# Probabilities times values by three split passes in the sparse attention, and eight steps of the adaptive-norm stream moved to the output projection

## The chip, the cores and the metric

The kernel runs on one core of one Trainium2 chip. The time is that of the device, in microseconds (us), median of several runs. The engines are called as in the profile: PE (TensorE, matrix products), PEld (its weight loads), DVE (VectorE), ACT (ScalarE), POOL (GpSimd) and SP, whose queue starts most DMAs.

## What is computed

One decoder layer over 512 tokens of width 2048, all in float32. Cut to what matters here:

```python
mod = silu(c) @ w_ada + b_ada            # six vectors of 2048: shift, scale, gate, twice
h = rms_norm(x) * (1 + sc_a) + sh_a
proj = h @ w_in                          # q, k, v of A; indexer; latents of B; two gates
score = sum_h relu(qi_h . ki) * wi_h     # indexer, 16 heads of 64; top 128 keys a row
p = softmax(where(selected, q . k * scale, -inf))
o_a = p @ v                              # mixer A: 8 heads of 128, v shared by 4 heads
o_b = causal attention                   # mixer B (MLA): 8 heads
y = (sigmoid(g_a) * (o_a @ w_pa) + sigmoid(g_b) * (o_b @ w_pb)) @ w_o
x = x + gt_a * y
x = x + gt_f * conv_ffn(rms_norm(x) * (1 + sc_f) + sh_f)
```

## The kernel before

Activations lie with 128 channels or tokens on the partitions and 512 tokens or channels along a row; a tile of that size is a slot, and 81 slots are handed out and given back by `get` and `put`. Products of activations with weights are made by split: each float32 operand becomes a high part in the reduced format fp32r and a low part, the rest (`split`: a copy on ACT, a subtraction on DVE), and `mm3` adds three fp32r passes, high by high, high by low and low by high (lines 166 to 168). Plain float32 products stand where an operand is used only once or twice: queries by keys (line 1023), and probabilities by values (line 813).

The stages in order of time: the combined input projection in quarters, to about 200 us; indexer and the rest of the projection, to about 420 us; mixer A, to about 570 us; gates, to 770; mixer B and the branch projections `w_pa` and `w_pb`, to 1077; the output projection `w_o`, to 1255; then the feed-forward network, the second half of the time.

**The indexer** (`index_heads`) takes three blocks of 128 query rows, of 256, 384 and 512 keys. Each block has eight calls of `two_rows` (line 638): two heads of 64 channels, in the upper and the lower half of the array, three passes each, so six half-height matmuls, which must keep their order. Around them PE works on the passes of the projection.

**Mixer A** loops over eight heads, one step out of phase: `attend_p` makes logits and softmax of a head, `attend_pv` transposes the probabilities of the head before (10 transposes, line 805), copies them out of PSUM (ACT and DVE by turns, lines 810 and 808), and multiplies them with the values, four matmuls of 512, 384, 256 and 128 columns (line 813). Between, `fill` gives PE one step of the gate projection at a time (24 passes of 512 columns), and calls `tick` after it.

**The stream of `w_ada`**: shift, scale and gate of the later sub-layers are sums over `w_ada`, made in 16 blocks of 8 steps, 128 steps in all. A step (`ada_load`, `ada_add`) loads two tiles of 256 KB by SP (line 837) and adds them, scaled, into an accumulator by two DVE instructions (lines 856 and 858). A `ticker` makes steps at a rate per call: in mixer A 1 and then 2 for each head, 27 in all; 20 each in the gates, with `w_pa` and with `w_pb`; in the output projection 1.25 (`TO`) for each of 32 calls, 40 in all. A finished block is summed over partitions by two passes with ones (`flush_cols`, lines 906 and 907).

The order on each engine is not the order of the code: a scheduler sets it when the kernel is built, by its own estimate of times and by priorities. Each engine then runs its queue in that order.

## Time and profile before

| | |
|---|---|
| median of 3 runs | 2592.22 us (2591.07 to 2593.68) |
| the profiled execution | 2595.53 us, of which its span is 2593.7 us |
| PE, DVE, ACT busy | 99%, 84%, 48% of the span |
| TensorE clock granted | 1.00 from 225 us to the end |

A matmul's record runs from its start to the modelled end of its pipeline, so records of one engine overlap. How fast PE works is read from start to start.

### The profile page before, as it was taken

The page shows a single profiled execution, that of the slowest core. Times are in us where ns is not written, and L with a number is a line of the kernel's source. Part 1 is how long each engine was busy: PE and PEld are TensorE (multiplying, and loading weights), DVE is VectorE, ACT ScalarE, POOL GpSimd, SP SyncE. Part 2 cuts the span into 40 slices and gives each one's busy share as a digit, 9 for nine tenths or more (in the row PEclk, how much of TensorE's full clock was granted, in tenths as well). Part 3 has the DMA queues.
Part 4 walks back from the last instruction along what each step waited for, and adds up shares of the span by engine and source line. Part 5 has one row for each costly group of instructions (what it writes and reads, how often), then busy time and mean ns, then how long its engine had stood idle before and what let it go on. Part 6 is the DMA issues. An engine that isn't in the chain of part 4 may idle for free.

```text
span 2593.7 us, 45167 instructions
## 1 busy us (share of the span) xinstructions
PE 2578.3 (99%) x17392; PEld 2341.9 (90%) x17392; DVE 2177.7 (84%) x3487; ACT 1241.1 (48%) x1949; POOL 371.3 (14%) x671
## 2 busy tenths in 40 slices
PE   9999999999999999999999999999999999999999
PEld 8887787779998877888889999999999999999999
DVE  6976995788878767876979989999989998989887
ACT  5322444344445535322545555555555555665554
POOL 1000011010023224200100000000000024414120
PEclk9999999999999999999999999999999999999999
DMA  9943136745685569966424334434344358868663
GB/s 342 362 155 110 48 100 190 228 151 175 203 269 166 161 209 352 320 230 226 154 81 156 128 122 130 141 120 133 126 150 136 126 169 230 225 167 228 155 204 116
DMA packets 216444, 466.41 MB, mean 180 GB/s; under 512 B 23930, under 2 KB 65556, under 8 KB 216228
## 3 DMA queue, kind: packets, MB, share of 16 engines
q1 hardware_dynamic: 170404, 344.93, 41.7%
q0 software_dynamic: 45792, 118.59, 15.2%
q8 instruction: 136, 2.23, 0.4%
q14 instruction: 80, 0.66, 0.1%
q10 hardware_dynamic: 32, 0.01, 0.0%
HBM read 398.16 MB, written 65.27 MB: 179 GB/s over the span
## 4 chain that ended last, share of the span: by engine, by line
PE 94%; issue 2%; DMA 2%; DVE 1%; ACT 1%; POOL 0%; SPq 0%; POOLq 0%; ACTq 0%; DVEq 0%
PE bank L1218 18%; PE bank L1220 18%; PE bank L1219 18%; PE bank L166 12%; PE bank L168 11%; PE bank L167 11%; PE bank L638 1%; PE bank L813 1%; PE bank L1366 1%; DMA raw<-in_w_ada 1%; PE bank L349 1%; PE bank L805 0%; DMA slot<-in_x 0%; DMA slot<-in_w_ada 0%; PE bank L1023 0%
## 5 line engine op out<-in xcount | busy, mean ns | idle before, releaser
L1218 PE MATMUL bank<-slot,whl 128*128 128x256 f32 x3920 | 1098.4, 281 | 3.1 <-ACT slot L1099 1.2
L1219 PE MATMUL bank<-slot,whl 128*128 128x256 f32 x3920 | 1097.0, 281 | 0.0
L1220 PE MATMUL bank<-slot,whl 128*128 128x256 f32 x3920 | 1084.9, 281 | 1.1 <-DVE whl L154 1.1
L1218 PEld LDWEIGHTS bank<-slot,whl 128*128 128x128 f32 x3920 | 737.3, 188 | 5.5 <-ACT slot L1099 2.3
L1219 PEld LDWEIGHTS bank<-slot,whl 128*128 128x128 f32 x3920 | 739.2, 189 | 0.2
L1220 PEld LDWEIGHTS bank<-slot,whl 128*128 128x128 f32 x3920 | 731.3, 188 | 1.6 <-DVE whl L154 1.5
L154 DVE TENSOR_TENSOR whl<-raw,whl 128x1024 fp32r<-128x1024 f32 (+2 forms) x560 | 607.8, 1088 | 126.9 <-ACT whl L153 121.6
L153 ACT ACTIVATE whl<-raw 128x1024 fp32r<-128x1024 f32 (+2 forms) x560 | 530.8, 949 | 357.9 <-PE bank L1219 187.9
L145 ACT ACTIVATE whl<-raw 128x1024 fp32r<-128x1024 f32 (+4 forms) x182 | 187.2, 1031 | 357.3 <-PE bank L168 182.8
L1095 DVE TENSOR_TENSOR raw<-raw 128x1024 f32<-128x1024 f32 (+2 forms) x320 | 347.1, 1085 | 3.6 <-DMA raw<-in_w_ups 1.3
L146 DVE TENSOR_TENSOR whl<-raw,whl 128x1024 fp32r<-128x1024 f32 (+4 forms) x182 | 215.6, 1187 | 111.9 <-ACT whl L145 111.1
L167 PE MATMUL bank<-whl,slot 128*128 128x512 f32 (+2 forms) x768 | 295.5, 385 | 0.0
L168 PE MATMUL bank<-whl,slot 128*128 128x512 f32 (+2 forms) x768 | 294.4, 386 | 0.0
L166 PE MATMUL bank<-whl,slot 128*128 128x512 f32 (+2 forms) x768 | 290.5, 389 | 1.5 <-DVE slot L1295 0.8
L167 PE MATMUL bank<-slot,whl 128*128 128x512 f32 (+1 forms) x656 | 263.5, 402 | 0.0
L166 PE MATMUL bank<-slot,whl 128*128 128x512 f32 (+1 forms) x656 | 261.3, 405 | 0.7 <-ACT slot L1548 0.7
L168 PE MATMUL bank<-slot,whl 128*128 128x512 f32 (+1 forms) x656 | 257.5, 401 | 0.0
L1101 ACT ACTIVATE slot<-bank 128x256 f32<-128x256 f32 x192 | 73.8, 385 | 210.5 <-PE bank L1220 210.5
L166 PEld LDWEIGHTS bank<-whl,slot 128*128 128x128 f32 x768 | 144.3, 188 | 31.0 <-issue 2.1
L168 PEld LDWEIGHTS bank<-whl,slot 128*128 128x128 f32 x768 | 144.3, 188 | 29.7 <-issue 2.2
L167 PEld LDWEIGHTS bank<-whl,slot 128*128 128x128 f32 x768 | 144.4, 188 | 29.0 <-issue 2.0
L858 DVE SCALAR_TENSOR_TENSOR slot<-slot,c_act,slot 128x512 f32<-128x512 f32 x203 | 150.8, 747 | 21.2 <-DMA slot<-in_w_ada 19.2
(296 smaller groups left out, 2774.7 us busy)
## 6 DMA issues: line engine op xcount, KB each, us to landing
slot<-in_w_ada SPq DMA_DIRECT2D x344, 256.0 KB, 5.3
raw<-in_w_ups SPq DMA_DIRECT2D x160, 512.0 KB, 3.6
raw<-in_w_in SPq DMA_DIRECT2D x50, 512.0 KB, 3.6
raw<-in_w_down SPq DMA_DIRECT2D x64, 384.0 KB, 4.0
raw<-in_w_down SPq DMA_DIRECT2D x64, 320.0 KB, 4.2
slot<-f POOLq DMA_DIRECT2D x154, 128.0 KB, 4.7
f<-slot POOLq DMA_DIRECT2D x66, 256.0 KB, 5.2
raw<-in_w_gs SPq DMA_DIRECT2D x32, 512.0 KB, 4.4
```

What stands on the lines that cost most here:

```text
L145: A.activation(hi, raw[:, :w], AF.Copy)
L146: last["lo"] = V.tensor_tensor(lo, raw[:, :w], r32(hi), ALU.subtract)
L153: return (A.activation(dst_hi, src, AF.Copy), V.tensor_tensor(dst_lo, src, r32(dst_hi), ALU.subtract))
L154: V.tensor_tensor(dst_lo, src, r32(dst_hi), ALU.subtract))
L166: PE.matmul(o, lh, rh, start=first, stop=False)
L167: PE.matmul(o, lh, rl, start=False, stop=False)
L168: PE.matmul(o, ll, rh, start=False, stop=last)
L858: V.scalar_tensor_tensor(acc, ts[i], c_act[:, k:k + 1], acc, op0=ALU.mult, op1=ALU.add)
L1095: V.tensor_tensor(o[:, :W], a[:, :W], b[:, :W], op)
L1218: PE.matmul(o, wh[:, ks], rh, start=first and k == 0, stop=False, skip_group_check=True)
L1219: PE.matmul(o, wh[:, ks], rl, start=False, stop=False, skip_group_check=True)
L1220: PE.matmul(o, wl[:, ks], rh, start=False, stop=last, skip_group_check=True)
```

## The change

The values of mixer A are split once into a high and a low part (`va`), and the tiles that held keys and values are given back at once. The transposed probabilities are split too, as they leave PSUM, into one set of three high and three low tiles for all heads, where before two heads had a set each of plain tiles. The four plain products of a head become twelve fp32r passes through `mm3`. Mixer B, which calls the same `attend_pv`, keeps the plain products. For heads 5 to 8 of the loop the first `fill` makes no step of the stream and the second makes one in place of two; `TO` goes from 1.25 to 1.5, which is 12 steps for each of the four column blocks of the output projection in place of 10.

```diff
-    TO=1.25,
+    TO=1.5,
...
+    va = ([getr(), getr()], [getr(), getr()])
+
+    def va_part(e, tb):
+        return va[e][tb // 2][:, (tb % 2) * 256:(tb % 2) * 256 + 256]
...
+        split(va_part(0, tb), va_part(1, tb), t[:, 256:512])
...
+    put(*kva)
...
-        att["t"] = [get() for _ in range(5)]
+        att["t"] = [getr() for _ in range(3)] if parts else [get() for _ in range(5)]
+        att["l"] = [getr() for _ in range(3)] if parts else []
...
+        if att["l"]:
+            pt, pl = [quad([*att[n][0:2], None, None, att[n][2]], 0) for n in "tl"]
+        else:
+            pt, pl = quad(att["t"], i), None
...
-            if kc % 2:
+            if pl:
+                last["cp"] = split(d, pl[3 - kc], b[:, :n])[1]
+            elif kc % 2:
...
-            PE.matmul(ob[:, kc * P:], vf(kc), pt[3 - kc], start=kc == 0, stop=kc == 3)
+            if pl:
+                mm3(ob[:, kc * P:], *vf(kc), pt[3 - kc], pl[3 - kc], kc == 0, kc == 3)
+            else:
+                PE.matmul(ob[:, kc * P:], vf(kc), pt[3 - kc], start=kc == 0, stop=kc == 3)
...
-    attend_bufs()
+    attend_bufs(True)
...
-        fill(1, 1)
+        fill(1, hd < 5)
...
-        fill(1, 2)
+        fill(1, 2 if hd < 5 else 1)
```

The built programs differ in order from the indexer to the end of the output projection; from the products with a unit matrix that spread the second norm (line 1533 before) PE's order is the same. Lines behind the first edits stand some lines later in the new program (858 before is 874 now, 1023 is 1039).

PE in mixer A, the products of the first head, between passes of the gate projection (whose rows name whl). Before:

```order
L813 MATMUL bank_73<-slot_3014,slot_409 128x512
L167 MATMUL bank_67<-slot_1007,whl 128x512
L168 MATMUL bank_67<-slot_1006,whl 128x512
L166 MATMUL bank_67<-slot_1011,whl 128x512
L1023 MATMUL bank_71<-slot_352,slot_130 128x384
L167 MATMUL bank_67<-slot_1012,whl 128x512
L813 MATMUL bank_73<-slot_3015,slot_412 128x384
L813 MATMUL bank_73<-slot_3600,slot_418 128x256
L813 MATMUL bank_73<-slot_3015,slot_280 128x128
```

Now, from its second product on:

```order
L167 MATMUL bank_73<-slot_3586,slot_2142 128x384
L168 MATMUL bank_73<-slot_3615,slot_2144 128x384
L166 MATMUL bank_73<-slot_3576,slot_2143 128x256
L167 MATMUL bank_73<-slot_3587,slot_2143 128x256
L168 MATMUL bank_73<-slot_3576,slot_2145 128x256
L166 MATMUL bank_73<-slot_3615,slot_2143 128x128
L167 MATMUL bank_73<-slot_3586,slot_2143 128x128
L168 MATMUL bank_73<-slot_3615,slot_2145 128x128
L1039 MATMUL bank_70<-slot_352,slot_2509 128x512
```

Four plain matmuls have become twelve passes. Between the first head's last transpose and its first product stand 21 gate passes, where there were 16.

PE in the indexer's last block (line 638, half-height, between passes of the projection), the third and fourth of its calls. Before:

```order
L638 MATMUL bank_72<-slot_1836,slot_2532 128x512
L638 MATMUL bank_71<-slot_1836,slot_2532 128x512
L638 MATMUL bank_72<-slot_1835,slot_1852 128x512
L638 MATMUL bank_71<-slot_1835,slot_1852 128x512
L638 MATMUL bank_70<-slot_1835,slot_2532 128x512
L638 MATMUL bank_73<-slot_1835,slot_2532 128x512
L638 MATMUL bank_70<-slot_1836,slot_2532 128x512
L638 MATMUL bank_73<-slot_1836,slot_2532 128x512
L638 MATMUL bank_70<-slot_1835,slot_1852 128x512
L638 MATMUL bank_73<-slot_1835,slot_1852 128x512
L168 MATMUL bank_66<-whl,slot_1327 128x512
```

Now the third of them:

```order
L168 MATMUL bank_66<-whl,slot_1332 128x512
L638 MATMUL bank_72<-slot_1835,slot_1866 128x512
L166 MATMUL bank_67<-whl,slot_1326 128x512
L638 MATMUL bank_71<-slot_1835,slot_1866 128x512
L638 MATMUL bank_72<-slot_1836,slot_1866 128x512
L638 MATMUL bank_71<-slot_1836,slot_1866 128x512
L638 MATMUL bank_72<-slot_1835,slot_2547 128x512
L638 MATMUL bank_71<-slot_1835,slot_2547 128x512
L167 MATMUL bank_67<-whl,slot_1326 128x512
```

Two calls that stood in one run of twelve now stand apart, and a full-height pass stands behind the first matmul of each, as in the four calls after them, so in six of the block's eight; before, three stood like that.

DVE in the last column block of the output projection, with the subtraction that makes each weight tile's low part (line 146) and the stream's additions between. Before:

```order
L146 TENSOR_TENSOR whl<-raw,whl 128x1024
L858 SCALAR_TENSOR_TENSOR slot_344<-slot_8785,c_act,slot_344 128x512
L858 SCALAR_TENSOR_TENSOR slot_344<-slot_8021,c_act,slot_344 128x512
L146 TENSOR_TENSOR whl<-raw,whl 128x1024
L858 SCALAR_TENSOR_TENSOR slot_344<-slot_6717,c_act,slot_344 128x512
L858 SCALAR_TENSOR_TENSOR slot_344<-slot_6745,c_act,slot_344 128x512
L146 TENSOR_TENSOR whl<-raw,whl 128x1024
```

Now, as far from the block's end:

```order
L146 TENSOR_TENSOR whl<-raw,whl 128x1024
L874 SCALAR_TENSOR_TENSOR slot_97<-slot_7145,c_act,slot_97 128x512
L872 TENSOR_SCALAR slot_280<-slot_6779,c_act 128x512
L874 SCALAR_TENSOR_TENSOR slot_97<-slot_7146,c_act,slot_97 128x512
L874 SCALAR_TENSOR_TENSOR slot_97<-slot_8847,c_act,slot_97 128x512
L874 SCALAR_TENSOR_TENSOR slot_280<-slot_6807,c_act,slot_280 128x512
L874 SCALAR_TENSOR_TENSOR slot_97<-slot_8083,c_act,slot_97 128x512
L874 SCALAR_TENSOR_TENSOR slot_280<-slot_7145,c_act,slot_280 128x512
L146 TENSOR_TENSOR whl<-raw,whl 128x1024
```

Between the last five subtractions of line 146 ahead of the block's results stood 2, 2, 5 and 5 additions; now 7, 3, 5 and 5.

## Rows read from the trace of the kernel before

**Rows 1.** The page: engines' busy time, and the chain that ended last.

```profile
PE 2578.3 (99%) x17392; PEld 2341.9 (90%) x17392; DVE 2177.7 (84%) x3487; ACT 1241.1 (48%) x1949; POOL 371.3 (14%) x671
PE 94%; issue 2%; DMA 2%; DVE 1%; ACT 1%; POOL 0%; SPq 0%; POOLq 0%; ACTq 0%; DVEq 0%
```

**Rows 2.** Waits of PE: line, releaser and its line, us in total, times, longest.

```profile
PE bank L166 <- DVE slot L1295: 0.8, 1, 0.8
...
PE bank L813 <- DVE slot L808: 0.2, 1, 0.2
```

**Rows 3.** Stretches: from:to length; busy PE, PEld, DVE, ACT, POOL; clock, DMA share, GB/s.

```profile
424.00:500.00 76.00, 75.84 (x336) 58.11 (x335) 62.14 (x143) 29.79 (x66) 5.92 (x11) 1.00 0.79 250
553.00:600.00 47.00, 47.00 (x210) 37.68 (x210) 43.54 (x82) 22.44 (x36) 4.30 (x8) 1.00 0.38 119
1077.00:1255.00 178.00, 178.00 (x782) 144.18 (x781) 129.15 (x175) 48.22 (x69) 4.72 (x8) 1.00 0.71 238
```

**Rows 4.** Order of time, PE, mixer A: start, us, engine, line, names, shape, count.

```profile
443.86 1.46 PE L813 MATMUL bank<-slot,slot 128*128 128x384 f32 x6
445.16 1.02 PE L1023 MATMUL bank<-slot,slot 128*128 128x512 f32 x2
...
457.62 1.02 PE L813 MATMUL bank<-slot,slot 128*128 128x512 f32 x2
...
458.48 0.81 PE L1023 MATMUL bank<-slot,slot 128*128 128x384 f32 x2
```

**Rows 5.** Order of time, PE: passes of 256 columns; plain products of one column.

```profile
1400.03 0.28 PE L1220 MATMUL bank<-slot,whl 128*128 128x256 f32 x1
1400.15 0.28 PE L1218 MATMUL bank<-slot,whl 128*128 128x256 f32 x1
...
80.14 0.95 PE L349 MATMUL bank<-c_act,slot 128*128 128x1 f32 x8
80.95 0.48 PE L168 MATMUL bank<-whl,slot 128*128 128x512 f32 x1
```

**Rows 6.** Order of time, PE, the indexer's last block.

```profile
315.98 0.40 PE L167 MATMUL bank<-whl,slot 128*128 128x512 f32 x1
316.30 1.66 PE L638 MATMUL bank<-slot,slot 64*128 64x512 f32 x12
...
318.23 0.40 PE L166 MATMUL bank<-whl,slot 128*128 128x512 f32 x1
...
321.29 0.40 PE L167 MATMUL bank<-whl,slot 128*128 128x512 f32 x1
321.62 0.49 PE L638 MATMUL bank<-slot,slot 64*128 64x512 f32 x1
322.04 0.51 PE L168 MATMUL bank<-whl,slot 128*128 128x512 f32 x1
322.48 0.97 PE L638 MATMUL bank<-slot,slot 64*128 64x512 f32 x5
...
323.72 0.40 PE L167 MATMUL bank<-whl,slot 128*128 128x512 f32 x1
323.95 0.39 PE L168 MATMUL bank<-whl,slot 128*128 128x512 f32 x1
324.18 0.39 PE L166 MATMUL bank<-whl,slot 128*128 128x512 f32 x1
324.50 0.96 PE L638 MATMUL bank<-slot,slot 64*128 64x512 f32 x6
...
325.73 0.40 PE L168 MATMUL bank<-whl,slot 128*128 128x512 f32 x1
```

**Rows 7.** By line, DVE: count, ns min/median/max, first and last start, forms.

```profile
L858 DVE SCALAR_TENSOR_TENSOR slot<-slot,c_act,slot x203: 728/746/754, 435.3 to 1248.5; 128x512 f32<-128x512 f32 x102
L808 DVE COPY slot<-bank x32: 281/413/559, 438.0 to 991.7; 128x384 f32<-128x384 f32 x16, 128x128 f32<-128x128 f32 x16
L154 DVE TENSOR_TENSOR slot<-bank,slot x15: 672/683/693, 234.6 to 918.1; 128x512 fp32r<-128x512 f32 x15
```

**Rows 8.** Order of time, DVE, the last steps of the output projection.

```profile
1244.17 1.23 DVE L146 TENSOR_TENSOR whl<-raw,whl 128x1024 fp32r<-128x1024 f32 x1 [0.53 <-ACT whl L145]
1245.31 3.90 DVE L858 SCALAR_TENSOR_TENSOR slot<-slot,c_act,slot 128x512 f32<-128x512 f32 x5
1249.73 1.23 DVE L146 TENSOR_TENSOR whl<-raw,whl 128x1024 fp32r<-128x1024 f32 x1 [0.52 <-ACT whl L145]
1250.87 1.28 DVE L1466 TENSOR_TENSOR slot<-bank,slot 128x512 f32<-128x512 f32 x2
```

More of the change, by code (lines that the diff above doesn't have):

```diff
@@ L763, in trunk_layer_kernel, with attend_bufs, attend_free @@
     att = {}
-    def attend_bufs():
+    def attend_bufs(parts=False):
         att["p"] = [get() for _ in range(5)]
-        att["t"] = [get() for _ in range(5)]
+        att["t"] = [getr() for _ in range(3)] if parts else [get() for _ in range(5)]
+        att["l"] = [getr() for _ in range(3)] if parts else []
         att["o"] = [getr() for _ in range(4)]
-    def attend_free(kinds="pto"):
+    def attend_free(kinds="ptlo"):
         for k in kinds:
@@ L791, in attend_p @@
         hcount[0] += 1
-        pq, pt = quad(att["p"], i), quad(att["t"], i)
+        pq = quad(att["p"], i)
         for qb in (3, 2, 1, 0):
@@ L797, in attend_p, with attend_pv @@
             soft(b[:, :S], pq[qb][:, :S], maskf(qb), nsc(qb))
-        return i, pq, pt, vf, dh, dl
-    def attend_pv(i, pq, pt, vf, dh, dl):
+        return i, pq, vf, dh, dl
+    def attend_pv(i, pq, vf, dh, dl):
+        if att["l"]:
+            pt, pl = [quad([*att[n][0:2], None, None, att[n][2]], 0) for n in "tl"]
+        else:
+            pt, pl = quad(att["t"], i), None
         for kc in range(4):
@@ L1025, in trunk_layer_kernel @@
             state = attend_p(qk, lambda qb: mask[qb], lambda qb, hd=hd: nsc_a[:, qb, hd:hd + 1],
-                             lambda kc, g=g: kva[kc][:, 256 + g * P:256 + (g + 1) * P], *oa_d[hd])
-        fill(1, 1)
+                             lambda kc, g=g: [va_part(e, kc)[:, g * P:(g + 1) * P] for e in range(2)], *oa_d[hd])
+        fill(1, hd < 5)
         if prev:
             attend_pv(*prev)
-        fill(1, 2)
+        fill(1, 2 if hd < 5 else 1)
         prev = state
@@ L1033, in trunk_layer_kernel @@
     put(*kaT)
-    put(*kva)
+    put(*va[0], *va[1])
     for t in qaT.values():
@@ L1368, in attend_pair @@
         for a in range(2):
-            attend_pv(a, pq[a], quad(att["t"], a), lambda kc, a=a: two(vv, kc)[:, a, :],
+            attend_pv(a, pq[a], lambda kc, a=a: two(vv, kc)[:, a, :],
                       *(ob_d[hp * 2 + a] if hp < 3 else (None, None)))
```

## The prediction

> **What bounds the kernel now.** I read the engines' busy time and the chain that ended last first: PE is busy for 99% of the span and carries 94% of the chain, and DVE, the next, is at 84% [rows 1]. Then the waits of PE: in the stretch that the change touches, mixer A to the output projection, there are seven, from 0.8 us down to 0.2 [rows 2], some 4 us together. The stretches say the same: from 424 to 500 us, where mixer A begins, PE is busy for 75.84 of 76 us beside a DVE at 62.14, and through the output projection for all of 178 us beside a DVE at 129.15 [rows 3]. So what counts is the time that PE itself takes for its queue, start to start, and beyond that only a wait so long that PE reaches it.
>
> **The products of mixer A.** A plain product is two records. The one of 512 columns takes from 457.62 to 458.48, 0.86 us, and those of 384, 256 and 128 columns together from 443.86 to 445.16, 1.30 us: 2.16 us a head [rows 4], 17.3 us for eight. Now there are twelve passes. One of 512 columns takes 0.23 us (323.72 to 323.95) [rows 6], one of 256 columns 0.12 us [rows 5], and one of 384 I put between them, at 0.175. No row has a full-height fp32r pass of 128 columns. From below it is half of the pass of 256, 0.06 us; from above it is a whole one, 0.12. The nearest row is one where the weights are 128 columns wide and almost nothing moves: eight records of one column in 0.81 us, 0.10 each [rows 5]. A pass of 128 columns loads as much, so I take 0.10. A head then takes 3 times 0.23, 0.175, 0.12 and 0.10, that is 1.88 us, and eight heads save 8 times 0.28, or 2.3 us; with the bounds 1.8 to 3.2.
>
> The Trainium skill, in "TensorE: Matmul & The Clock Gate", section "LDWEIGHTS (loading the stationary operand)", has the load of weights cost their columns over 1.2 a nanosecond, which is 107 ns for 128 columns however little is streamed. It speaks against the narrow passes: by it the saving would be 2.1 us, and if streaming alone counted 3.2. The rows of one column agree with it at 0.10 us.
>
> **What the scheduler did to the indexer.** Values and keys leave their slots earlier and a split stands ahead of the indexer's heads, and the order on PE has changed there, though the indexer's own work has not. This costs PE time. A call of six half-height matmuls in one piece, at 324.50, takes from the start of the full pass ahead of it (324.18) to the second one behind (325.73) 1.55 us; less the two passes at 0.23, 1.09. A call with one full pass behind its first matmul takes 2.43 us (321.29 to 323.72), less three passes 1.74: 0.65 more. Two calls in one run of twelve take 2.25 (315.98 to 318.23), less two passes 1.79, against twice 1.09: 0.39 saved [rows 6]. In the block of 512 keys three calls were broken like that and two stood together; now six are broken and none stand together: 3 times 0.65 and 0.39, 2.3 us. In the block of 384 keys one more call is broken and two more stand together: between nothing and 0.26 us, and I take 0.15, since a narrower call loses less. The block of 256 keys, and the same pattern in mixer B, are as they were. Together 2.5 us lost, with bounds of 2.3 and 2.6.
>
> **The engines beside.** The four tiles that leave PSUM cost ACT two more copies a head, and DVE four subtractions in place of two copies. The subtraction of 512 columns takes 0.68 us, the copies 0.28 at 128 and 0.56 at 384 [rows 7]; with 0.55, 0.42 and 0.30 estimated for the narrower ones, DVE gets 1.95 us for 0.84, 1.1 us more a head. About five heads begin in the 76 us from 424, so DVE goes there from 62 to some 67.5 us, 89%, and PE has at least the 21 gate passes of 0.23 us between transposes and products, 4.8 us, as cover. For the values four subtractions of 256 columns, some 1.7 us, lie in the indexer under the projection's passes. If the cover fails, PE waits for each subtraction in turn; that is the second rival.
>
> Each of the eight steps that go is two additions of 0.75 us [rows 7], two DMAs of 256 KB on SP and their queue entries: 12 us of DVE and 4.2 MB. In heads 5 to 8 this more than pays for the splits, and it eases the time from 553 to 600 us, where DVE was busy for 43.54 of 47 us [rows 3]. Eight steps are one block, so every later sum over partitions comes one block later, at the same point of a block, and as many passes with ones are made. In the output projection DVE goes from 129 to 141 of 178 us and the DMAs from 238 to some 262 GB/s [rows 3]; the slots of the ring are handed on by additions, the weights of `w_o` and `w_up` stand behind them in SP's queue, and at 79% DVE has time to hand them on. At the end 20 additions stand in the last four steps where 14 stood. At the rows' rate, 3.90 us for five and 1.14 for the weight subtraction ahead of them [rows 8], that is 15.6 and 4.6 us, 20.2 of the four steps' 22.3 (24 passes of 0.23 us each). So the first result, which was taken at 1250.87 [rows 8], comes as early as now. The single set of tiles for the split probabilities makes a head's copies wait for the products of the head before; in PE's order those stand ahead of the transposes that feed the copies, or level with them.
>
> **The sum.** On PE 2.3 us less and 2.5 us more: 0.2 us more, with bounds of 0.9 less and 0.8 more. The profiled execution took 2595.53 us, which gives 2595.7; it stood 3.3 us above the median, and from the median of 2592.22 it is 2592.4. What a measurement of this kernel can tell from no change is about 0.2%, 5 us. The forecast is the same time.
>
> **The rivals.**
> 1. The products gain what they can and the broken calls cost little, because on the chip the pass between may find its weights loaded earlier. For it: the saving of 1.8 to 3.2 us is PE's own and nothing stands beside it. Against: in the rows each of the broken calls costs its 0.65 us. Time: 2592.2 less 3, 2589.2.
> 2. Slower: the chain of four copies and four subtractions isn't through when PE comes to the products. DVE takes its queue in order, so a subtraction stands behind the softmax of the next head, and behind what else comes due, such as five additions and a weight subtraction, 5.0 us [rows 8], against a cover of 4.8. For it: 89% on DVE. Against: the products waited 0.2 us in all for the copies of line 808 [rows 2], and the scheduler has put five more passes between. It decides when DVE is late by more than the cover at most heads; at 1 us a head, 8 us: 2600.
> 3. The additions in the output projection come late, since their DMAs do, and hold up the weights or the results behind them: the 2.1 us that the last four steps leave are gone, and PE waits for some 2 us at the end. 2594.5.
> 4. The waits that PE has, some 4 us, fall away with the new order beside the saving of 3: 2585.
> 5. The change doesn't do what it says: passes of 128 columns run at the plain price, two records of 0.11 us, as some reduced rate for narrow ones would make it. A head would take 2.24 us, not less than before: 0.6 more in place of 2.3 less, 2595.3.
>
> **How the numbers follow.** The forecast gets 0.60, the rivals in their order 0.16, 0.09, 0.07, 0.05 and 0.03. The forecast alone would hold from 2590 to 2595: bounds of the sum and a microsecond or two by which the runs differ. The range takes in the first, the third and the fifth rival, 2588.5 to 2596.5. Faster by over 0.2% is the fourth and a little of the first, 0.06; slower by over 0.2% is the second, 0.09; within it 0.85.
>
> **What the profile will show.** The twelve passes at 0.23, 0.175, 0.12 and 0.10 us, 1.9 us a head; six broken calls in the indexer's last block; no wait on the subtractions that is longer than a few tenths; DVE near 67 us from 424 to 500 and near 141 in the output projection; PE idle no longer there than before. The prediction is wrong if PE waits for the split probabilities at each head, if the narrow passes take much less or more than 0.10 us, if a broken call costs PE nothing, or if a wait appears after 1255 us, where PE's order is the same.

## The result and the profile after

The changed kernel takes 2612.55 us (median of 6 runs, 2608.49 to 2617.76) where the kernel before takes 2592.39: a ratio of 1.0079, interval 1.0069 to 1.0089. It is slower by 20 us, and the forecast of no change is wrong.

The page of the changed kernel, busy time, then the chain by engine and by line:

```profile
PE 2585.1 (99%) x17424; PEld 2348.9 (90%) x17424; DVE 2185.1 (84%) x3507; ACT 1245.1 (48%) x1969; POOL 373.0 (14%) x671
PE 89%; DMA 5%; DVE 4%; issue 1%; ACT 1%; SPq 0%; POOL 0%; DVEq 0%; POOLq 0%; ACTq 0%
PE bank L1234 17%; PE bank L1236 17%; PE bank L1235 17%; PE bank L166 11%; PE bank L168 11%; PE bank L167 11%; DMA slot<-in_w_ada 3%; PE bank L638 1%; DMA raw<-in_w_ada 1%; DVE slot L874 1%; DVE whl L146 1%; PE bank L829 1%; PE bank L816 1%
```

Beside [rows 1], busy shares are the same. But the chain has moved: PE carries 89% of it, not 94%, and DMA 5% where it carried 2%, 3% of it loads of `w_ada` into slots. The additions of the stream (line 874 now) and the subtractions of the weights (line 146) stand in it with 1% each. PE's waits, longest in total first, with times and the longest:

```profile
PE bank L167 <- DVE whl L146: 3.5, 2, 3.2
PE bank L1236 <- DVE whl L154: 3.2, 2, 2.7
...
PE bank L166 <- ACT slot L739: 1.7, 1, 1.7
PE bank L1498 <- ACT slot L1505: 1.5, 1, 1.5
...
PE bank L166 <- DVE slot L1346: 0.8, 1, 0.8
```

Before, the longest between mixer A and the output projection was 0.8 us [rows 2]. The stretches of [rows 3], and then four short ones around the two longest waits (columns as there):

```profile
425.00:500.00 75.00, 74.48 (x346) 58.78 (x345) 61.94 (x147) 32.49 (x74) 6.49 (x13) 1.00 0.77 243
553.00:600.00 47.00, 47.00 (x211) 38.43 (x210) 38.55 (x63) 20.12 (x31) 4.29 (x8) 1.00 0.44 135
1077.00:1255.00 178.00, 174.80 (x756) 141.08 (x755) 139.35 (x194) 48.72 (x69) 8.35 (x14) 0.98 0.80 263
...
750.00:760.00 10.00, 7.33 (x57) 7.13 (x56) 5.55 (x7) 2.84 (x4) 1.25 (x3) 0.94 0.76 244
760.00:770.00 10.00, 10.00 (x69) 9.62 (x68) 5.86 (x9) 3.76 (x6) 5.68 (x11) 0.89 1.05 336
...
1090.00:1098.00 8.00, 4.80 (x21) 3.59 (x20) 6.12 (x10) 3.18 (x3) 0.50 (x1) 0.91 1.04 326
1098.00:1104.00 6.00, 6.00 (x16) 4.65 (x16) 5.70 (x8) 0.00 (x0) 0.00 (x0) 0.55 1.04 384
```

PE lacks 3.2 us in the output projection, and where it has waited the granted clock is below 1.00 for some microseconds after. There the loss is larger than the wait.

**By stage.** The order at the start and in the feed-forward network is the same in all kernels here, so the time between two landmarks tells where it went. Landmarks on PE: the first record of line 381 (31.6 to 39.5 us), the first queries by keys of mixer A, the first and the last Strassen pass of the gates, mixer B's last transpose, the products of line 1533, the last record. What lies before line 381 differs from execution to execution, since the clock rises earlier or later: from 20 to 30 us the granted clock was 0.72 in the profiled execution before and 1.00 in the one after. Hence the table begins behind it. First line in us, then differences from it; the last column is the timed median less that of the kernel before on the same chip.

```
kernel          indexer,  mixer A  gates   mixer B  w_pb,   feed-    sum     timed
                project.                            w_o     forward
before           387.5    177.6    161.7   228.1    267.3   1331.5   2553.8
changed           +5.6     -2.1     +5.0    +1.6     +7.0     +2.4    +19.5   +20.2
e1_split          +5.1     -2.7     +1.6    -2.6     -0.1     +2.9     +4.2    +6.9
e2_move           +0.4     -0.7     +2.8    +3.9     +5.7     +0.7    +12.8   +11.5
e3_ring           +5.1     -3.2     +1.9    +3.6    +12.6     +1.0    +21.0   +21.3
e4_gates          +5.1     -3.0    +21.2    +3.0     +5.5     +4.5    +36.2   +35.6
e5_late           +5.6     -5.3     +1.9    -2.8      0.0     +2.5     +1.9    +2.6
e6_rate            0.0     -0.3     +2.0    +1.9     +6.9     +5.4    +16.0   +18.8
e7_back            0.0     +0.7     +9.2    -0.4     -1.2     -0.5     +7.8    +7.1
e8_qa            +19.4     -2.7     +2.1    -0.8     +0.2     +3.4    +21.6   +23.3
e9_bufs           +0.8     -3.2     +3.2    -1.8     +0.1     +2.1     +1.1    +0.7
e11_both         +19.7     -2.0     +4.7    +1.3     +6.9     +0.9    +31.4   +30.1
f1_late_o         +5.1     -3.2     +5.1    +1.1     +0.5     +2.4    +11.0   +13.0
f4_gate_end       +5.4     -3.2     +2.8    +2.2     +2.8     +0.6    +10.6   +12.1
f5_all            +0.7     -3.5     +4.9    +5.5     +0.9     +1.0     +9.5    +8.7
f6_split_gate     +0.7     -3.2     +3.9    +7.8     -0.3     +0.4     +9.5    +6.4
```

The sums agree with the timed medians within 3.1 us, so the traces hold the loss. The feed-forward network's column tells nothing of the change: at the same order its passes come slower or faster evenly over the whole stage, by 0.5 us less to 4.5 more in all. (In e6_rate the 5.4 us are lost up to 1332 us, 2.3 of them in a wait for a sum of the steps left over.)

**The two longest waits.** DVE before and behind 750 us, in order of time (start, us, line, names, count, idle time before and its releaser):

```profile
745.15 1.22 DVE L1111 TENSOR_TENSOR raw<-raw 128x1024 f32<-128x1024 f32 x1
747.28 0.75 DVE L874 SCALAR_TENSOR_TENSOR slot<-slot,c_act,slot 128x512 f32<-128x512 f32 x1 [0.91 <-DMA slot<-in_w_ada]
747.95 2.36 DVE L154 TENSOR_TENSOR whl<-raw,whl 128x1024 fp32r<-128x1024 f32 x2
754.76 0.75 DVE L874 SCALAR_TENSOR_TENSOR slot<-slot,c_act,slot 128x512 f32<-128x512 f32 x1 [4.45 <-DMA slot<-in_w_ada]
755.43 1.22 DVE L1111 TENSOR_TENSOR raw<-raw 128x1024 f32<-128x1024 f32 x1
756.56 1.22 DVE L154 TENSOR_TENSOR whl<-raw,whl 128x1024 fp32r<-128x1024 f32 x1
```

and PE there:

```profile
754.77 0.28 PE L1234 MATMUL bank<-slot,whl 128*128 128x256 f32 x1
754.89 0.28 PE L1235 MATMUL bank<-slot,whl 128*128 128x256 f32 x1
757.84 0.39 PE L1236 MATMUL bank<-slot,whl 128*128 128x256 f32 x1 [2.67 <-DVE whl L154]
...
759.44 0.41 PE L1234 MATMUL bank<-slot,whl 128*128 128x256 f32 x1
759.65 0.41 PE L1235 MATMUL bank<-slot,whl 128*128 128x256 f32 x1
```

One addition waits 4.45 us for its transfer; the combination and the subtraction of the next weights stand behind it in DVE's queue, and PE waits for those. From 758.8 to 762.0 the passes of 256 columns then start 0.21 us apart, not 0.12: half the clock. Of the loads of `w_ada` into slots that were issued between 725 and 747 us, eight queue entries, one needed 8.9 us to land, the middle one 3.2; before, none over 4.0.

The start of the output projection, DVE again, then PE:

```profile
1084.17 1.22 DVE L146 TENSOR_TENSOR whl<-raw,whl 128x1024 fp32r<-128x1024 f32 x1
...
1089.58 0.75 DVE L874 SCALAR_TENSOR_TENSOR slot<-slot,c_act,slot 128x512 f32<-128x512 f32 x1
...
1091.62 2.33 DVE L874 SCALAR_TENSOR_TENSOR slot<-slot,c_act,slot 128x512 f32<-128x512 f32 x3
1095.75 0.75 DVE L874 SCALAR_TENSOR_TENSOR slot<-slot,c_act,slot 128x512 f32<-128x512 f32 x1 [1.80 <-DMA slot<-in_w_ada]
1096.42 2.35 DVE L146 TENSOR_TENSOR whl<-raw,whl 128x1024 fp32r<-128x1024 f32 x2
```

```profile
1097.69 0.79 PE L167 MATMUL bank<-whl,slot 128*128 128x512 f32 x1 [3.20 <-DVE whl L146]
...
1098.71 0.63 PE L166 MATMUL bank<-whl,slot 128*128 128x512 f32 x1
1099.13 0.63 PE L167 MATMUL bank<-whl,slot 128*128 128x512 f32 x1
```

Between two subtractions of weights, at 1084 and 1096 us, stand seven additions, the last of which waits 1.80 us for its transfer; another had waited 5.0 us at 1070. PE waits 3.2 us, and the thirteen passes from 1097.69 to 1103.40 take 5.7 us in place of 3.0, the most of them 0.43 us apart and not 0.23. Seven additions stand between two subtractions there before the change as well. What is new is that they wait. DVE's waits for loads of `w_ada` into slots, 1060 to 1098 us (us in total, times, longest), of which the kernel before has none in this stretch and 1.2 us right behind it:

```profile
DVE slot L874 <- DMA slot<-in_w_ada: 6.8, 2, 5.0
DVE slot L872 <- DMA slot<-in_w_ada: 1.4, 1, 1.4
```

### The profile page after: what moved, and what is told of

Read it like the earlier page. It is cut to its first block, busy times and chain, and to the rows that moved or that the text cites. A ratio compares the mean times of both kernels' runs of the same rounds, so it can differ in the third digit from the quotient of the medians.

```text
span 2608.9 us, 45286 instructions
## 1 busy us (share of the span) xinstructions
PE 2585.1 (99%) x17424; PEld 2348.9 (90%) x17424; DVE 2185.1 (84%) x3507; ACT 1245.1 (48%) x1969; POOL 373.0 (14%) x671
## 4 chain that ended last, share of the span: by engine, by line
PE 89%; DMA 5%; DVE 4%; issue 1%; ACT 1%; SPq 0%; POOL 0%; DVEq 0%; POOLq 0%; ACTq 0%
PE bank L1234 17%; PE bank L1236 17%; PE bank L1235 17%; PE bank L166 11%; PE bank L168 11%; PE bank L167 11%; DMA slot<-in_w_ada 3%; PE bank L638 1%; DMA raw<-in_w_ada 1%; DVE slot L874 1%; DVE whl L146 1%; PE bank L829 1%; PE bank L816 1%; PE bank L1382 1%; DMA slot<-in_x 0%
```

## The experiments

Theories at the outset: **A**, the move is the loss, at those two places; **B**, the split is, because PE now comes at another time to the same transfers. "Stream" is the stream of `w_ada`.

**e1_split and e2_move: each part alone.** From some 680 us, in the middle of the gates, the orders of e1_split are those of the kernel before, and those of e2_move are those of the changed kernel. Between mixer A and there each differs a little, in the places of additions and combinations on DVE, so the expectation of e1_split is not right in that.

```diff
# e1_split, from the changed kernel          # e2_move, from the kernel before
-    TO=1.5,                                 -    TO=1.25,
+    TO=1.25,                                +    TO=1.5,
-        fill(1, hd < 5)                     -        fill(1, 1)
+        fill(1, 1)                          +        fill(1, hd < 5)
-        fill(1, 2 if hd < 5 else 1)         -        fill(1, 2)
+        fill(1, 2)                          +        fill(1, 2 if hd < 5 else 1)
```

> The three split passes alone; the ada steps stay where they were before the change. After the end of the sparse attention the order on every engine is that of the kernel before. Theory A (the loss of 20 us is the move's: the ada stream runs eight steps late from the sparse attention to the output projection, and in two places an addition that waits for its transfer now stands ahead of weight halves in VectorE's queue): the sparse attention gains 2.1 us, the broken calls of the indexer's last block lose 2.3 us, and nothing else changes: 2592.6 us, between 2590.5 and 2595; no TensorE wait over 1 us around 750 or 1095. Theory B (the loss is the split's: TensorE comes some us earlier or later to the same transfers and meets them unfinished): the waits at 750 and 1095 are here too, 2605 us or more.

> The move of the eight ada steps alone, with the plain products in the sparse attention as before the change. Theory A: nearly all of the loss is here: 2592.4 + 20 - 0.2 = 2612 us, between 2606 and 2616, with a TensorE wait for the whl halves of about 3 us near 750 and another near 1095, and a low granted clock right behind each. Theory B: 2592 to 2596 us, and neither wait.

Measured: e1_split 2600.95 us, ratio 1.0025 (1.0015 to 1.0035); e2_move 2605.63, ratio 1.0040 (1.0027 to 1.0053). The parts add up to the whole, 17.0 of 19.5 us in the traces. The move has both waits (1.7 us at 753, 2.7 at 1093), the split neither, as A has it; but the split costs 5.1 us ahead of mixer A, where theory A had only the 2.3 of the broken calls. There PE waits for ScalarE's evacuation of a query bank. ACT in e1_split, in order of time:

```profile
339.95 0.69 ACT L752 ACTIVATE slot<-bank,col 128x512 f32<-128x512 f32 x1 [3.40 <-DVE slot L687]
340.99 0.60 ACT L739 ACTIVATE slot<-bank 128x512 f32<-128x512 f32 x1 [0.35 <-DVE slot L688]
```

The evacuation (line 739) stands behind a copy that waits 3.4 us for a slot that the indexer's scan (line 687) still uses. Before, the values stayed where they were, and no copy there waited for line 687: four slots taken a little earlier have dealt out all the later ones anew. In the changed kernel it is the same wait of 1.7 us at 341.

**e5_late, e8_qa, e9_bufs: the value splits elsewhere.** The split alone, as in e1_split; the four splits behind the projections (e5_late), behind the queries' projection (e8_qa), or behind the buffers of mixer A (e9_bufs).

```diff
-        split(va_part(0, tb), va_part(1, tb), t[:, 256:512])     # inside the loop over keys
-    put(*kva)
...
+    va = ([getr(), getr()], [getr(), getr()])                    # at the new place
+    for tb in range(4):
+        split(va_part(0, tb), va_part(1, tb), kva[tb][:, 256:512])
+    put(*kva)
```

> The split alone, as in e1_split, but the four splits of the values stand behind the queries' projection in place of inside the indexer's last block. In the trace of e1_split that block and the projections behind it lost 5.1 us: TensorE visits cut in two, and a wait of 1.7 us on ScalarE's evacuation of a query bank. Theory A (these 5.1 us are the place of the value splits, not the split products): most of it goes, the sparse attention keeps its gain of 2.7 us, and the time is 3 to 5 us under that of e1_split: 2596 to 2598 us, if the kernel before is at 2594. Rival B (the splits at the head of the sparse attention hold up its first products, and the slots they take make others wait): as slow as e1_split or slower, 2601 us or more, with a TensorE wait over 1 us between 420 and 440.

> The split alone, as in e1_split, with the four value splits behind the queries' projection: other slots than in e5_late, and the indexer's visits are as whole as in the kernel before (50 runs of half-height matmuls on TensorE, 54 in e1_split). From the sparse attention on the order is that of e1_split. Theory A (what e1_split lost before the sparse attention is the four cut visits and the wait of 1.7 us on the evacuation of a query bank, and nothing else stands against the gain of 2.3 to 2.7 us of the passes): 5 us less than e1_split and 2 us less than the kernel before: 2591 us, if that is at 2593. Rival B (the split products gain nothing on the whole, because what TensorE gains there it waits for later): 2593 to 2595 us, with the 2.3 us lost again in the gates of the Strassen stage.

> The split alone, with the value splits behind the allocation of the attention's buffers, at the head of the sparse attention; whole visits as in e8_qa. Theory A: 2591 us, as e8_qa. Rival C (the splits at this place, eight instructions of 0.6 to 0.7 us, stand ahead of the first products and TensorE waits for them): 2592 to 2594 us, with a TensorE wait of 1 us or more at the first product with the split values, near 440.

Measured: 2595.58 (1.0010, 1.0002 to 1.0019), 2616.34 (1.0093, 1.0079 to 1.0108) and 2593.83 (1.0007, 0.9997 to 1.0016). e5_late came, in its time, close to its theory A. e9_bufs is the clean one: PE's runs of half-height matmuls are 50 as before, where e1_split has 54 and e5_late 55; up to the end of mixer A nothing waits, and it is 2.4 us ahead of the kernel before (+0.8 and -3.2). That is what the passes give. e5_late doesn't wait there either and is 0.3 us behind the kernel before: 2.7 us for the broken calls alone. e9_bufs loses 1.4 of them in gates and mixer B, and the timing can't tell it from the kernel before: rival B of e8_qa's expectation, a gain that is given back, seen on another kernel. e8_qa missed by 25 us, for the reason seen in e1_split. Its ACT row:

```profile
378.80 0.44 ACT L991 ACTIVATE slot<-bank 128x320 f32<-128x320 f32 x1 [15.10 <-DVE slot L687]
```

The latents' evacuation got a slot of the indexer's scan and waited 15.1 us for it, PE 16.7, and the clock fell behind it (0.63 from 379 to 386 us). The place of four small splits decides between 1 and 23 us, not through their own 1.7 us of DVE but through the slots that others get and the order on PE.

**e3_ring and e4_gates: later additions.** The changed kernel with more distance between a load and its addition.

```diff
# e3_ring
-                while len(loaded) > 2 * ada_ring_on[0]:
+                while len(loaded) > 3 * ada_ring_on[0]:
-    ada_ring.extend(get() for _ in range(6))
+    ada_ring.extend(get() for _ in range(8))
# e4_gates
-                while len(loaded) > 2 * ada_ring_on[0]:
+                while len(loaded) > (2 if ada_ring_on[0] else ada_in_slots[0]):
```

> The changed kernel with a ring of eight slots in place of six and additions three steps behind their loads in place of two, from the mixer B output to the output projection, so that an addition finds its transfer landed. Theory C (what stalls TensorE near 1095 is the addition that waits for in_w_ada ahead of the weight halves in VectorE's queue: 3.2 us of wait, and about 2.8 us at half the clock behind it): both go, about 6 us less than the changed kernel, 2606 us, and if the rest of the 7 us lag between 1000 and 1250 is of the same kind 2605; the loss near 750 stays. Rival D (the DMA engines are full there, with a share of 0.97 to 1.05, so the weights themselves are late, and a deeper ring takes more of the same bandwidth): 2610 to 2615, with TensorE waiting for the halves as long as before.

> The changed kernel with each ada addition one step behind its load while the loads go to free slots (the gates of the sparse attention and the Strassen stage), in place of right behind it. Theory C (the wait near 750 is an addition that waits 4.5 us for in_w_ada ahead of the halves): the TensorE wait of 2.7 us and the low clock behind it go, 4 to 5 us less than the changed kernel, about 2608 us; the loss near 1095 stays. Rival D (the transfers are late whatever stands behind them, or the order shifts elsewhere): 2611 to 2616, with a wait of the same kind at another place.

Measured: 2615.43 (1.0077, 1.0064 to 1.0090) and 2629.72 (1.0137, 1.0122 to 1.0152). In e3_ring the wait near 1095 is gone, PE is busy there for 20.00 of 20 us; but three others have come, of 1.2 to 1.5 us, at 999, 1001 and 1013 us, where `w_pb` begins, and the one at the end of the stage has grown from 1.5 to 3.7 us, at 1276:

```profile
1000.00:1020.00 20.00, 16.51 (x57) 12.31 (x58) 14.61 (x22) 10.38 (x17) 7.59 (x14) 0.83 1.03 370
1080.00:1100.00 20.00, 20.00 (x88) 16.18 (x87) 16.71 (x26) 6.08 (x8) 8.86 (x15) 1.00 1.03 345
```

e4_gates waits 4.4 us at 618 and 3.1 at 631, at the head of the gates, and loses 21 us there; its wait near 757 is 0.8 and 1.1 us at two places. So theory C was right about the single wait in each and wrong about the time. More distance was no repair in either: it moves every later addition too.

**e6_rate and e7_back: where the eight steps run.** The move alone, with the old rate in the output projection, so that eight steps are left for its end (e6_rate), or made up for in the gates (e7_back).

```diff
-    TO=1.5,
+    TO=1.25,
# e7_back also
-    TS=0.36,
+    TS=0.50,
```

> The move alone, as in e2_move, but at the rate of before in the output projection: 1.25 steps a tick in place of 1.5, so that the eight steps are left over and run at its end. Theory S (the loss comes from the stream's being eight steps behind everywhere, whatever the rate): until the output projection nothing changes, and the TensorE wait of 2.7 us near 1095 with its stretch of low clock is still there. Theory L (the loss of 5.7 us between 1000 and 1260 is the larger load of additions and transfers in the output projection): that wait goes, and about 4 us of it. In both the eight steps left over cost at its end: 8 x 1.5 = 12 us of VectorE, of which up to 10 show: 2606 to 2618 us.

> The move alone, as in e2_move, but the eight steps are made up in the gates of the Strassen stage (0.50 steps a tick in place of 0.36) and not in the output projection, where the rate is that of before. Theory S: from the dense attention on the stream is where it was before the change, so the 3.9 us lost in the dense attention and the 5.7 us lost from 1000 to 1260 go; the gates lose what eight more steps of 1.5 us on a busy VectorE cost, between the 2.8 us of e2_move and 8: 2596 to 2602 us where the kernel before has 2594. Theory L (TensorE's losses follow the number of additions per stage): the gates lose more than 8 us, 2602 us or more, while the later stages lose nothing.

Measured: 2611.80 (1.0076, 1.0060 to 1.0091) and 2600.13 (1.0028, 1.0016 to 1.0039). e6_rate has no wait near 1095, and DVE stands there for 3.0 us where it stands for 7.7 in e2_move: that wait goes with the old rate, as theory L has it, but not because fewer additions stand ahead of it (the table below: 18 and 19); its own 6.9 us are lost at the end, 1.4 and 4.9 us of waits at 1258 and 1263. In e7_back, where the stream has caught up by the end of the gates, nothing is lost behind them, theory S; but the gates lose 9.2 us, in six waits of 0.5 to 2.4 us, three of 0.2 and a granted clock of 0.51 from 755 to 758 us. The time lies in S's range, the gates' loss in L's.

**f1_late_o and f4_gate_end: the two places mended.** The changed kernel with the eight steps in the last three quarters of the output projection, and with no step in the last 12 of the gates' 56 Strassen steps.

```diff
# f1_late_o
-        tick, step = ticker(TO), [0]          # TO=1.5
+        tick, step = ticker(TO if db else 1.25), [0]   # TO=1.6
# f4_gate_end
-        gate_tick()                           # TS=0.36
+        if q < n - 12:
+            gate_tick()                       # TS=0.46
```

> The changed kernel with the eight moved steps taken later in the output projection: 1.25 steps a tick in its first quarter, as before the change, and 1.6 in the other three in place of 1.5 in all four. In the trace of the kernel before, the first quarter has the DMA engines at a share of 0.96 to 1.05 and VectorE busy 15 to 18 us of 20, and the stretch from 1120 to 1240 has a share of 0.35 to 0.95 and VectorE 11 to 14. Theory L (the wait of 3.2 us near 1095 and the half clock behind it come from more additions and loads where the transfers are full): both go, 5 to 6 us less than the changed kernel: 2607 us where the kernel before has 2593. Theory S (the shift of the stream is enough, wherever the eight steps run): the wait stays, 2612 us.

> The changed kernel with no ada step in the last 12 of the 56 steps of the Strassen stage of the gates, and 0.46 a tick in place of 0.36 in the 44 before, so that the stream enters the dense attention where it did. In the changed kernel TensorE waits 2.7 us near 757 for the halves behind an addition whose transfer takes 8.9 us from issue to landing, and runs at a granted clock of 0.89 to 0.94 behind it. Theory C (that one addition, ahead of the halves in VectorE's queue among the reloads for the dense attention, costs these 4 to 5 us): the wait and the low clock go and the gates take 162 to 164 us in place of 166.7; 2608 to 2610 us where the kernel before has 2593. Rival D (the stage has no room for the steps: what is taken from its end is lost earlier, at 0.46 a tick): the gates take 166 us or more, with waits for the halves spread over 620 to 720.

Measured: 2605.16 (1.0049, 1.0034 to 1.0064) and 2604.23 (1.0051, 1.0035 to 1.0068): 13.0 and 12.1 us above the kernel before, where the changed kernel is 20.2 above it. In f1_late_o the stage of `w_pb` and `w_o` loses 0.5 us in place of 7.0, and the wait near 1095 is gone, as theory L forecast:

```profile
1090.00:1104.00 14.00, 14.00 (x62) 11.28 (x61) 12.93 (x17) 4.89 (x5) 0.00 (x0) 1.00 1.01 343
```

DVE is busier there than in the changed kernel and the transfers as full (1.01), and its longest bunch is one of eight additions. So it does not have more room. But it stands less for transfers, in the stretch of 1060 to 1098 us:

```profile
DVE slot L874 <- DMA slot<-in_w_ada: 4.7, 5, 2.4
```

All sixteen kernels: DVE's waits there for `in_w_ada` into slots (lines 872 and 874 of the changed kernel and their like); PE's wait near 1095 for the weights behind them; and the additions in DVE's queue between seven subtractions of weights (line 146), the last of them the one at 1096 us in the changed kernel, for which PE waits there:

```
                                 DVE's      PE's    additions between
                                 waits, us  wait    the subtractions   sum
before, four split-only kernels  0 to 1.3   0       2 1 3 3 1 7        17
e6_rate, e7_back                 3.0, 4.4   0       2 1 2 5 1 7        18
f6_split_gate                    6.7        0.6     2 1 2 5 1 7        18
f1_late_o, f5_all                4.7, 5.0   0       2 1 2 5 1 8        19
e3_ring                          5.2        0       4 2 3 3 2 7        21
f4_gate_end                      5.8        1.9     2 2 2 3 3 7        19
e2_move                          7.7        2.7     2 2 2 3 3 7        19
e4_gates (22 us later)           7.8        2.6     2 2 2 3 3 7        19
e11_both (21 us later)           8.1        3.2     2 2 2 3 3 7        19
changed                          8.2        3.2     2 2 2 3 3 7        19
```

The five kernels in which PE waits for 1.9 us or more are the five with one order on DVE. The number of additions doesn't decide it: f1_late_o has as many and e3_ring more. Within that order PE waits the longer, by and large, the longer DVE stands. Where DVE stands for up to some 5 us, the subtractions, which run ahead of PE, take it up. Whether the order acts by the standing alone is not separated here; f6_split_gate, with 6.7 us in another order and 0.6 on PE, speaks against it.

f4_gate_end:

```profile
750.00:760.00 10.00, 10.00 (x87) 10.00 (x87) 6.08 (x7) 4.46 (x6) 3.20 (x6) 1.00 0.71 206
...
1090.00:1104.00 14.00, 12.11 (x53) 9.51 (x52) 11.75 (x15) 3.33 (x4) 0.00 (x0) 1.00 1.00 357
```

The wait near 757 is gone, as theory C says; the gates are shorter by 2.2 us only. Of the gates' 1344 Strassen passes the last 200 take 4.1 us more in the changed kernel than in the kernel before, and 0.8 less in f4_gate_end; those ahead of them 0.9 more in the changed kernel, and 3.6 more here, with waits of 0.2 to 0.5 us between 667 and 735. That part is rival D's: more than half of what the end gave back is lost earlier. The larger gain, 4.2 us, was in neither expectation: in the output projection, whose order on DVE is that of the changed kernel, PE waits 1.9 us and not 3.2, and the clock stays at 1.00. So at one order the size of a wait still differs with what has gone before.

**e11_both, f5_all, f6_split_gate: taken together.** e11_both is the changed kernel with the value splits of e8_qa; f5_all is split and move with the repairs of e9_bufs, f1_late_o and f4_gate_end; f6_split_gate is e9_bufs with the edit of f4_gate_end. No line in them is new.

> The changed kernel, split and move, with the value splits behind the queries' projection as in e8_qa; the orders on SyncE and GpSimd are the same as in the changed kernel, and TensorE's differ only up to the end of the queries' projection. Theory A (the two parts of the loss add up): the indexer's 5 us go and the move's 12 to 15 us stay: 2606 to 2608 us where the kernel before has 2593, with the waits near 750 and near 1095 as in the changed kernel. Rival D (TensorE's arrival decides whether it meets the transfers late, so that an earlier or later start of 5 us moves or removes the waits): anything from 2596 to 2615, with waits at other places.

> Split and move, with the three repairs together: the value splits behind the buffers of the sparse attention as in e9_bufs, the eight steps in the last three quarters of the output projection as in f1_late_o, no ada step in the last 12 steps of the gates as in f4_gate_end. Theory A (the loss is these three places): from the changed kernel's 20 us above before go 5 for the value splits, 7 for the output projection and 2 to 5 for the gates: 2595 to 2598 us where the kernel before has 2592. Rival B (the move itself costs, because eight additions more in any later stage meet a VectorE that is three quarters busy): 2600 us or more.

> The split alone as in e9_bufs, with no ada step in the last 12 steps of the gates and 0.46 a tick before. Theory A (the lead of 2.4 us that the passes give is lost at the end of the gates, to an addition that waits for its transfer): the lead stays, 2590 us where the kernel before has 2592, and the gates take 162 us. Rival B (the lead is absorbed anyway, by transfers or by the busier stretch before): 2592 to 2594 us.

Measured: 2623.13 (1.0115, 1.0100 to 1.0131), 2601.77 (1.0031, 1.0019 to 1.0043) and 2599.47 (1.0021, 1.0011 to 1.0030). e11_both has e8_qa's 16.7 us ahead of mixer A, so its expectation fell with that one's. What it shows all the same: with PE some 20 us later than in the changed kernel, the waits near 757 and 1095 are there still, 2.0 and 3.2 us where they were 2.7 and 3.2, and the stage of `w_o` loses 6.9 us as before. That speaks against B: the waits go with the order on DVE, not with the time of PE's arrival, which at most changes their size. f5_all keeps 8.7 of the 20 us, as its rival B forecast: the three waits are gone, but gates and mixer B lose 10.4. f6_split_gate missed both of its theories: mixer B loses 7.8 us, with waits of 2.3 us at 776 and 1.9 at 947, where the kernel before waits 0.8 and 0.6, and a low clock in both stretches:

```profile
770.00:790.00 20.00, 17.74 (x92) 16.07 (x91) 16.34 (x55) 9.70 (x25) 6.50 (x9) 0.91 0.70 221
940.00:960.00 20.00, 18.08 (x73) 12.11 (x72) 8.61 (x17) 5.50 (x11) 3.79 (x8) 0.91 0.85 260
```

It has not moved a step to another stage; its stream is only spaced otherwise within the gates. The wait near 945 has come with that spacing: it is 1.7 to 1.9 us in the three kernels that have it, and at most 0.6 in the kernel before, the changed kernel and e9_bufs. No version here beats the kernel before.

## Why the prediction was wrong

By its own steps:

- **The passes: right.** Forecast 2.3 us gained, 1.88 us a head. The twelve passes of a head in one piece, in the changed kernel:

```profile
465.71 0.40 PE L166 MATMUL bank<-slot,slot 128*128 128x512 f32 x1
...
467.27 0.22 PE L166 MATMUL bank<-slot,slot 128*128 128x128 f32 x1
467.33 0.27 PE L167 MATMUL bank<-slot,slot 128*128 128x128 f32 x1
467.44 0.27 PE L168 MATMUL bank<-slot,slot 128*128 128x128 f32 x1
467.55 2.15 PE L1039 MATMUL bank<-slot,slot 128*128 128x512 f32 x6
```

  From 465.71 to 467.55 is 1.84 us; the three narrow passes take 0.06, 0.11 and 0.11. e9_bufs shows the whole gain, 2.4 us. By an estimate from the Trainium skill's page "TensorE: Matmul & The Clock Gate", section "LDWEIGHTS (loading the stationary operand)", the three would take 0.32 us; the rows have 0.28, since the first load (467.16) lies under the wider pass ahead. No wait stands on the subtractions of the split probabilities: rival 2 fell.
- **The broken calls: right.** Six calls in the indexer's last block, as foreseen. The stretch up to mixer A's end costs 4.8 us more in e1_split than in e9_bufs; 2.0 of them are PE's idle time, which leaves 2.8 against 2.5; e5_late, which doesn't idle there, loses 2.7 to e9_bufs.
- **"For the values four subtractions ... lie in the indexer under the projection's passes": the first step that failed.** It priced the splits' time, 1.7 us of DVE, and not the four slots. Sized nothing, measured 2.0 us here, and 16.7 in e8_qa.
- **"At 79% DVE has time to hand them on": the step that failed most.** 79% is a mean over 178 us. The same view of the kernel before, cut in three:

```profile
1000.00:1077.00 77.00, 77.00 (x333) 62.30 (x333) 72.62 (x107) 33.51 (x51) 18.97 (x34) 1.00 0.93 321
1077.00:1123.00 46.00, 46.00 (x200) 37.19 (x199) 39.70 (x56) 11.91 (x16) 2.54 (x4) 1.00 0.89 307
1123.00:1255.00 132.00, 132.00 (x583) 106.99 (x583) 89.45 (x120) 36.31 (x54) 2.18 (x4) 1.00 0.64 214
```

  The first quarter follows on a stretch with DVE at 94%, is itself at 86% with the transfers at 0.89, and the rest is at 68% and 0.64. The load was as forecast, 139 us of DVE (141) and 263 GB/s (262) in the whole stage. But a busy share says nothing of the time for which DVE stands for a transfer with a weight's subtraction behind it: 8.2 us from 1060 to 1098, before none. And it was not the eight steps' own load that did it: up to the subtraction for which PE waits at 1096 us stand 19 additions where 17 stood, in another order, and f1_late_o has 19 as well, with no wait of PE. Most of the steps added come later, where DVE had room. Sized nothing; 7.0 us, and 0.5 in f1_late_o. I looked at the queue at the end of the stage, where 20 additions had to fit; the loss was at its start.
- **"Every later sum ... comes one block later, at the same point of a block": the third.** It followed the sums and not the additions, whose places between the weights' subtractions changed through gates and mixer B. Sized nothing; 6.6 us in the changed kernel, 6.7 in e2_move. In the changed kernel 4.1 of the 6.6 are lost at the end of the gates, with the wait near 757. That an order can do this without any step moved to another stage f6_split_gate shows: it loses 11.7 us there, where e9_bufs, which differs from it in that spacing alone, loses 1.4.
- **No term for the clock.** Each wait was priced at its length. Near 1095 the changed kernel lost 3.2 us to the wait and 2.7 to the passes behind it.

Rival 3 had the mechanism, additions that come late with their transfers and hold up the weights behind them, but at the end of the stage, at 2 us and a chance of 0.07. The signs that the prediction named came in part: a wait after 1255 us, 1.5 us at 1270, none at the heads of mixer A. DVE was foreseen at 67 us from 424 to 500 and is at 61.94 (from 425): the subtractions come as foreseen, some 1 us more a head than the copies, but of the stream's additions 30 (line 874) fall into the stretch, where 38 (line 858) did.

Open: why one load took 8.9 us where its like took 3.2; why e9_bufs gives back 1.4 of its 2.4 us (its order in the first half of the gates isn't that of the kernel before); which rows make gates and mixer B lose 10 us in f5_all, beside the wait near 945. The waits are in the traces, their causes were not tried one by one.

## What to carry to other kernels

Where an engine takes its queue in order, ask of each instruction that waits for a transfer what stands behind it and who needs that, and read the room of engine and transfers in stretches as short as the work that stands ahead, not over a stage: a busy share leaves out the time for which the engine stands. Work that is moved shifts everything of its kind that follows until the stream has caught up, and a buffer taken earlier deals out all later buffers anew: both are to be followed to their end, also where neither load nor count has changed. When a kernel has been fitted like this one, a gain of 0.1% on the bounding engine is less than what a new order may cost.

## What the hardware showed

- **A wait costs more than its length, not always.** After 3.2 us without work (1094.5 to 1097.7) passes of 512 columns started 0.43 us apart until 1103.4, which is 1.2 in place of 2.4 GHz (granted clock 0.50 from 1098 to 1103); after 2.7 us, at 757, those of 256 columns 0.21 apart for 3.2 us, but after about a microsecond at full speed. After 1.9 us at 1093 in f4_gate_end the granted clock stayed at 1.00. In e3_ring 3.2 us at 781 were followed by no low clock either. So length alone doesn't decide it.
- **The start differs by the clock.** The time to line 381 lay between 31.6 and 39.5 us in executions with the same order, and was longest where the granted clock was low: from 20 to 30 us it was 0.58 in e4_gates (39.3 us), 0.72 before (36.5), 1.00 in the changed kernel (32.1). Up to eight microseconds of that kind lie in a comparison of two profiled spans. Here it is four: the execution before was a long one, so the spans differ by 15 us where the medians differ by 20.
- **The narrowest passes.** fp32r of 128 columns and 128 rows of weights: the next pass starts 0.06 us behind one whose load lies under a wider pass ahead, and 0.11 behind one that follows another narrow one. But the 0.06 are not its price. One that stands alone between passes of 512 columns:

```profile
519.09 0.22 PE L166 MATMUL bank<-slot,slot 128*128 128x128 f32 x1
519.15 0.44 PE L166 MATMUL bank<-slot,whl 128*128 128x512 f32 x1
519.43 0.39 PE L167 MATMUL bank<-slot,whl 128*128 128x512 f32 x1
```

  The pass behind takes 0.28 us in place of 0.23, and its load starts only at 519.09, with the narrow pass. Together the narrow pass has cost 0.11, which is also how far apart the loads start where narrow passes follow each other (467.16, 467.27 and 467.38).
